# A hybrid recurrent layer on one core: the mixers' steps emitted by an estimated clock of each engine

## The chip, the core and the metric

The kernel runs on one core of a Trainium2 chip. The core has a matrix engine (TensorE, PE in the profile), a vector engine (VectorE, DVE), a scalar engine (ScalarE, ACT), a general engine (GpSimd, POOL) and SyncE (SP), whose queue issues most DMAs; each engine runs its own instructions in order and waits on the others through semaphores. The metric is the device time of one execution in microseconds.

## The reference

One layer on a prompt of 512 tokens and a sample of 64, model width 2048, all in float32. What is computed, cut to what matters:

```python
def gla_step(s, blk):                      # 4 heads, dk 128, dv 256
    q, k, v, g = blk
    big_g = jnp.cumsum(g, axis=2)
    ...
    attn = jnp.einsum('bhid,bhjd,bhijd->bhij', q, k, decay)
    o = (jnp.einsum('bhij,bhjv->bhiv', attn, v)
         + jnp.einsum('bhid,bhdv->bhiv', q * jnp.exp(big_g), s))
    ...
def gdn_step(s, blk):                      # 8 heads, dk = dv = 128
    q, k, v, g, beta = blk
    ...
    lower = jnp.where(strict, jnp.einsum('bhid,bhjd->bhij', kb, k) * decay, 0.0)
    sol = lax.linalg.triangular_solve(eye + lower, rhs, left_side=True, lower=True,
                                      unit_diagonal=True)
    u = sol[..., :dv] - jnp.einsum('bhik,bhkv->bhiv', sol[..., dv:], s)
    o = (jnp.einsum('bhid,bhdv->bhiv', q * jnp.exp(big_g)[..., None], s)
         + jnp.einsum('bhij,bhjv->bhiv', attn, u))
    ...
def trunk(x, c, states, params, block):
        mod = jax.nn.silu(c) @ w_ada[l] + b_ada[l]
        sh1, sc1, g1, sh2, sc2, g2 = jnp.split(mod[:, None, :], N_MOD, axis=-1)
        h = rmsnorm(x, norm1[l]) * (1 + sc1) + sh1
        mix, s_a, s_b, s_c = token_mixers(h, ...)   # h @ w_in, conv + silu on GDN's q/k/v,
                                                    # gla_step, gdn_step, norms, gates, @ w_out
        x = x + g1 * mix
        h = rmsnorm(x, norm2[l]) * (1 + sc2) + sh2
        f, s_f = conv_ffn(h, ...)                   # w_up, causal conv, silu * val, w_down
        x = x + g2 * f
```

## The kernel before

The stages follow each other on TensorE. The head (0 to 197 us) computes the first two modulation vectors, the norm and its transposes. Then come 50 tiles of the input projection, `gdn_heads` (31) and `gla_heads` (19); then the output projection, its second half of rows (k from 8) first; then the FFN and the last norm. Weights arrive in float32 (`raw`), ScalarE rounds them to `wh` and VectorE takes the rest as `wl` (L650 to L652); a product is three matmuls, high times high, low times high and high times low (L564, L566). Prompt and sample form 2 x 288 columns, so one *gemm step* is six matmuls of 128x288, and a tile has 16 steps.

After each gemm step `K.tick` runs, 928 times in all. A tick takes one step of the oldest job that has something to do, and steps of the modulation stream. A job is a generator: `gdn` for each delta-rule head (and one for the samples), `gla` for each gated head. It yields `WAIT` when it has nothing to issue. Before, it says how many ticks to wait by constants, such as these:

```python
REST_S, REST_L, REST_D, REST_X, REST_U, REST_T, REST_H, REST_N, REST_O, REST_G = 2, 3, 6, 4, 12, 2, 2, 4, 4, 4
LAG_CONV, LAG_COPY = 11, 5
ADA_AHEAD = 2
```

`gdn` transposes (L157), forms the strictly lower matrix (L227), and inverts it: `inverse16` writes it to DRAM (L372), reads the diagonal 16x16 blocks so that they lie on lanes (L378), eliminates them on POOL (a chain of 14 pairs), writes back (L389), reads (L393) and unpacks them on VectorE with a mask (L398). Two levels of matmuls (L249, then a mask product on VectorE, then L255 and an addition on VectorE), and for the heads a third (L263, L269), double the blocks; between two of them lies a *hop*, TensorE to VectorE and back, in which TensorE should have gemm steps to run. Norms add a constant on VectorE (L150) and raise to a power on POOL. `_Sooner` (L1710) gives the jobs' instructions a higher priority in the scheduler; `_InTurn` (L1725) keeps POOL's instructions in the order in which they were emitted. SP's queue holds weight loads (L650), modulation weight loads (L812), and the DRAM trips in the scheduler's order.

The modulation stream `ada_blocks` computes the four other modulation vectors on VectorE: 512 KB of `w_ada` (tile `aw`, L812), four multiply-adds on it (L848, L850), and after 8 loads a sum by TensorE (L822). It gets 0.72 of a step each tick, and its pauses use up steps too. `gdn_conv` (a convolution of four taps on VectorE, L990, and SiLU on ScalarE, L994) and `gla_gate` are called at once at the end of their projection tile, all their instructions together.

## Time and profile before

| | us |
|---|---|
| median of 3 runs (lowest, highest) | 2925.44 (2918.93, 2926.12) |
| the profiled execution | 2921.86 |
| its span, first to last instruction | 2920.1 |
| TensorE busy | 2823.8 (97%) |
| VectorE busy | 2051.2 (70%) |
| ScalarE busy | 1182.5 (40%) |
| GpSimd busy | 311.7 (11%) |

The granted clock of TensorE was 0.987 of full speed in the mean. All 128 loads of `aw`, 512 KB each, go through SP's queue. In the views `PE L255 <- POOL m L1725` reads: an instruction of line 255 on TensorE stood, and the last event before it started was POOL's on a tile named m, from line 1725. Buffers and names of one kind share a name (`m` is a pool of tiles of 128x512). A time in square brackets is the idle time of the engine before that instruction. `SPq` is SP's queue.

### The profile page before, as it was taken

Reading aid. Unit: us, or ns where it says so; the run is one execution under the profiler, and the core shown is the slowest. Engines: PE = TensorE matmul, PEld = TensorE weight load, DVE = VectorE, ACT = ScalarE, POOL = GpSimd, SP = SyncE. Lnnn points to the kernel's source line nnn. Section 1 sums busy time; section 2 is a strip of 40 time slices with the busy share of each in tenths; the row PEclk is TensorE's granted clock in tenths of the full one; section 3 lists DMA queues with packets and bytes.
Section 4 is the critical chain, followed back from the end, with each engine's and each line's share of the span. In section 5 each row is a group of like instructions: output and inputs, shape, how many; then the busy total and the mean of one; then the engine's idle time right before and its main releaser. Section 6 shows DMA issues by size and latency. Waiting matters only on the chain.

```text
span 2920.1 us, 52016 instructions
## 1 busy us (share of the span) xinstructions
PE 2823.8 (97%) x20964; PEld 2734.4 (94%) x20964; DVE 2051.2 (70%) x3299; ACT 1182.5 (40%) x2032; POOL 311.7 (11%) x513
## 2 busy tenths in 40 slices
PE   6999989999899999999999999999999999999998
PEld 3688889999899998999999999999999999999997
DVE  3368666777568787578888888888888855555555
ACT  4234534555454343255444444444444421222223
POOL 0005141222200000000111111111111100000000
PEclk8999999999999999999999999999999999999999
DMA  8865544555444548633333334333333553323221
GB/s 267 283 204 150 161 133 138 149 150 161 135 131 144 155 118 231 184 119 96 106 111 107 102 104 116 109 99 107 109 109 106 181 185 97 119 96 120 80 81 66
DMA packets 535444, 395.53 MB, mean 135 GB/s; under 512 B 59657, under 2 KB 465412, under 8 KB 535204
## 3 DMA queue, kind: packets, MB, share of 16 engines
q1 hardware_dynamic: 527860, 390.54, 44.7%
q8 instruction: 165, 2.70, 0.4%
q10 hardware_dynamic: 7344, 1.67, 0.3%
q14 instruction: 75, 0.61, 0.1%
HBM read 356.47 MB, written 35.67 MB: 134 GB/s over the span
## 4 chain that ended last, share of the span: by engine, by line
PE 80%; DVE 6%; POOL 4%; issue 4%; DMA 3%; ACT 2%; SPq 1%; ACTq 0%; POOLq 0%; DVEq 0%
PE g L564 26%; PE g L566 13%; PE bank L1388 11%; PE bank L1387 11%; PE bank L1389 11%; POOL m L1725 3%; DVE acc L850 1%; PE bank L724 1%; PE bank L157 1%; PE bank L441 1%; DVE wl L652 1%; DVE ca L990 1%; DVE m L1710 1%; ACT m L1710 1%; DMA d<-m 1%
## 5 line engine op out<-in xcount | busy, mean ns | idle before, releaser
L1388 PE MATMUL bank<-slot,wh 128*128 128x290 f32 x2464 | 737.3, 299 | 0.0
L1387 PE MATMUL bank<-slot,wh 128*128 128x290 f32 x2464 | 733.2, 298 | 0.0
L1389 PE MATMUL bank<-slot,wl 128*128 128x290 f32 x2464 | 728.2, 296 | 0.0
L564 PE MATMUL g<-slot,wh 128*128 128x288 f32 x3168 | 552.7, 295 | 0.2 <-DVE slot L1157 0.2
L564 PE MATMUL g<-hh,wh 128*128 128x288 f32 x2048 | 476.6, 313 | 1.0 <-ACT wh L651 1.0
L1389 PEld LDWEIGHTS bank<-slot,wl 128*128 128x128 f32 x2464 | 470.6, 191 | 0.0
L1388 PEld LDWEIGHTS bank<-slot,wh 128*128 128x128 f32 x2464 | 468.7, 190 | 0.1
L564 PEld LDWEIGHTS g<-slot,wh 128*128 128x128 f32 x3168 | 464.5, 188 | 0.7 <-DVE slot L1157 0.5
L1387 PEld LDWEIGHTS bank<-slot,wh 128*128 128x128 f32 x2464 | 463.6, 188 | 0.1
L651 ACT ACTIVATE wh<-raw 128x1024 fp32r<-128x1024 f32 x215 | 227.6, 1058 | 539.1 <-PE g L564 507.0
L564 PE MATMUL g<-hl,wh 128*128 128x288 f32 x2048 | 445.1, 298 | 0.0
L566 PE MATMUL g<-hh,wl 128*128 128x288 f32 x2048 | 443.7, 297 | 0.0
L1157 DVE SCALAR_TENSOR_TENSOR slot<-g,mod,slot 128x512 f32<-128x512 f32 (+1 forms) x448 | 201.6, 491 | 268.5 <-PE g L566 267.7
L564 PEld LDWEIGHTS g<-hh,wh 128*128 128x128 f32 x2048 | 328.4, 191 | 20.8 <-issue 16.3
L850 DVE SCALAR_TENSOR_TENSOR acc<-aw,ct,acc 128x512 f32<-128x512 f32 x480 | 337.7, 750 | 10.2 <-DMA aw<-in_w_ada_dram 10.2
L566 PE MATMUL g<-slot,wl 128*128 128x288 f32 x1584 | 342.6, 295 | 0.0
L566 PEld LDWEIGHTS g<-hh,wl 128*128 128x128 f32 x2048 | 331.6, 190 | 6.2 <-issue 6.2
L564 PEld LDWEIGHTS g<-hl,wh 128*128 128x128 f32 x2048 | 332.4, 190 | 3.6 <-issue 3.5
L652 DVE TENSOR_TENSOR wl<-raw,wh 128x1024 fp32r<-128x1024 f32 x215 | 262.6, 1222 | 64.6 <-ACT wh L651 64.0
L1334 ACT ACTIVATE wh<-raw 128x1024 fp32r<-128x1024 f32 x176 | 186.2, 1058 | 224.2 <-PE bank L1388 182.3
L566 PEld LDWEIGHTS g<-slot,wl 128*128 128x128 f32 x1584 | 256.1, 188 | 0.0
L1335 DVE TENSOR_TENSOR wl<-raw,wh 128x1024 fp32r<-128x1024 f32 x176 | 215.3, 1223 | 54.0 <-ACT wh L1334 54.0
(351 smaller groups left out, 3102.2 us busy)
## 6 DMA issues: line engine op xcount, KB each, us to landing
raw<-in_w_up_dram SPq DMA_DIRECT2D x176, 512.0 KB
aw<-in_w_ada_dram SPq DMA_DIRECT2D x128, 512.0 KB
raw<-in_w_in_dram SPq DMA_DIRECT2D x100, 512.0 KB
raw<-in_w_down_dram SPq DMA_DIRECT2D x88, 512.0 KB
hraw<-in_w_ada_dram SPq DMA_DIRECT2D x64, 512.0 KB
raw<-in_w_out_dram SPq DMA_DIRECT2D x32, 512.0 KB
slot<-actd SPq DMA_DIRECT2D x44, 288.0 KB
actd<-v SPq DMA_DIRECT2D x44, 256.0 KB
```

The source lines that it names most:

```text
L564: T.matmul(ps[:, h if bank is None else bank, :n], wh, x[:, h, :n], start=f, stop=False)
L566: T.matmul(ps[:, h if bank is None else bank, :n], wl, ah[:, h, :n], start=False, stop=stop)
L651: nc.scalar.activation(hi[:, :n_], raw[:, :n_], AF.Copy)
L652: nc.vector.tensor_tensor(lo[:, :n_], raw[:, :n_], hi[:, :n_].bitcast(F32), op=ALU.subtract)
L850: V.scalar_tensor_tensor(acc[s], w[:, k], col, acc[s], op0=ALU.mult, op1=ALU.add)
L1157: self.nc.vector.scalar_tensor_tensor(x1[:, :, z], ps[:, :, c], gain[:, q:q + 1], x1[:, :, z], op0=ALU.mult, op1=ALU.add)
L1334: self.nc.scalar.activation(hi, src, AF.Copy)
L1335: self.nc.vector.tensor_tensor(lo, src, hi.bitcast(F32), op=ALU.subtract)
L1387: T.matmul(ps, wh[:, j], hi, start=(c < 3 and j == 0), stop=False, skip_group_check=True)
L1388: T.matmul(ps, wh[:, j], lo, start=False, stop=False, skip_group_check=True)
L1389: T.matmul(ps, wl[:, j], hi, start=False, stop=(j == NPAIR - 1), skip_group_check=True)
L1725: r = f(*a, **kw)
```

## The change

Two constants for each engine (a fixed price and a price per element), 0.795 us for a gemm step and prices for a DMA make a planner's clock. `K.now` is TensorE's, `K.free` has the time at which each other engine should be through with what was emitted, and each job has a `chain`, the planned end of its last instruction. `until` yields `WAIT` until TensorE's clock has passed the chain, `hop` does so after a yield, `moved` puts a DMA's price on the chain, `wait_for` waits for a tile's planned time. All counts of ticks go. The four taps of `gdn_conv` and the parts of `gla_gate` become tasks that run over several ticks and call `done` with a planned time; the jobs wait for q and k by it. The modulation stream takes a step only while VectorE's planned backlog is below 1 us; credit of 0.72 a tick is kept, up to 200 steps, and waits use none. Its weights have two buffers in place of three, and the pool m 17 in place of 15. The GLA jobs and the samples start their steps once at most one GDN job is left. `_Sooner` and `_InTurn` stay.

```diff
-REST_S, REST_L, REST_D, REST_X, REST_U, REST_T, REST_H, REST_N, REST_O, REST_G = 2, 3, 6, 4, 12, 2, 2, 4, 4, 4
-REST_C = 11
-REST_V = 5
-LAG_CONV, LAG_COPY = 11, 5
-ADA_AHEAD = 2
+TICK_US, HOP_US, DMA_US, ISSUE_US = 0.795, 0.25, 2.6, 0.5
+ADA_BACKLOG, ADA_CREDIT = 1.0, 200.0
+OP_US = {"V": (0.12, 1 / 960.0), "A": (0.10, 1 / 960.0), "G": (0.30, 1 / 480.0)}
+ADA_AHEAD = 1
...
-        self.jv, self.ja = _Sooner(tc, tc.nc.vector), _Sooner(tc, tc.nc.scalar)
-        self.pool = _InTurn(tc, tc.nc.gpsimd)
+        self.now, self.chain, self.free = 0.0, None, dict.fromkeys(OP_US, 0.0)
+        self.jv, self.ja = _Timed(self, _Sooner(tc, tc.nc.vector), "V"), _Timed(self, _Sooner(tc, tc.nc.scalar), "A")
+        self.tv, self.ta = _Timed(self, tc.nc.vector, "V"), _Timed(self, tc.nc.scalar, "A")
+        self.jt = _TimedPE(self, tc.nc.tensor)
+        self.pool = _Timed(self, _InTurn(tc, tc.nc.gpsimd), "G")
...
+    def rsqrt_steps(self, out, src, n):
+        self.rsqrt(out, src, n)
+        yield from self.until()
...
-        yield from self.rest(REST_C)
+        yield from self.wait_for(x, "q")
+        yield from self.wait_for(x, "k")
...
-        self.rsqrt(rq, ss, 4)
+        yield from self.until()
+        yield from self.rsqrt_steps(rq, ss, 4)
         V.tensor_scalar_mul(rq, rq, float(P) ** -0.5)
-        yield from self.rest(REST_T)
+        self.chain = at
+        yield from self.hop()
...
-                yield from self.hop(0)
+                yield from self.hop()
...
+    def charge(self, key, n, extra=0.0):
+        base, per = OP_US[key]
+        start = max(self.free[key], self.now + HOP_US, self.chain or 0.0)
+        self.free[key] = end = start + base + per * n + extra
+        if self.chain is not None:
+            self.chain = end
+    def charge_pe(self, us):
+        self.now += us
+        if self.chain is not None:
+            self.chain = max(self.chain, self.now)
+    def wait_for(self, x, name):
+        while name not in x or self.now < x[name, "at"]:
             yield WAIT
-        V.tensor_tensor(kF, kF, x["gate"](), op=ALU.mult)
-        yield from self.rest(REST_O)
-        o_put(kF)
-    def ready(self, x, name):
-        return name in x and self.ticks >= x.get((name, "at"), 0)
-    def put_ready(self, x, name, get, lag):
-        x[name], x[name, "at"] = get, self.ticks + lag
+    def put_ready(self, x, name, get, at):
+        x[name], x[name, "at"] = get, at
...
-    def rest(self, n):
-        for _ in range(n):
+    def until(self):
+        while self.now < self.chain + HOP_US:
             yield WAIT
-    def hop(self, n=REST_H):
+    def hop(self):
         yield
-        yield from self.rest(n)
+        yield from self.until()
+    def moved(self, n=1):
+        self.chain = max(self.chain, self.now) + DMA_US + n * ISSUE_US
...
-        yield from self.rest(REST_S)
+        yield from self.until()
...
+        self.moved(4)
+        yield from self.until()
...
-        yield from self.rest(REST_X)
+        self.moved(2)
+        yield from self.until()
         t, u = self.m4(), self.m4()
         for w, x in enumerate((t, u)):
-            nc.vector.tensor_tensor(x.rearrange("p b (n j) -> p b n j", n=8), cm[:, w].unsqueeze(2).to_broadcast(sh),
+            self.tv.tensor_tensor(x.rearrange("p b (n j) -> p b n j", n=8), cm[:, w].unsqueeze(2).to_broadcast(sh),
                                     c["bd16"].rearrange("p (n j) -> p n j", n=8).unsqueeze(1).to_broadcast(sh), op=ALU.mult)
-        yield from self.rest(REST_U)
+        yield from self.hop()
...
+    def fewer(self, n):
+        while sum(j[0].__name__ == "gdn" for j in self.jobs) > n:
+            yield WAIT
+    def start(self, gen, at=0.0):
+        self.jobs.append([gen, max(at, self.now)])
+    def spawn(self, gen):
+        self.tasks.append([gen, self.now])
+        self.run_tasks(self.tasks[-1:])
+    def run_tasks(self, tasks):
+        for j in tasks:
+            self.chain = j[1]
+            done = next(j[0], self) is self
+            j[1], self.chain = self.chain, None
+            if done:
+                self.tasks.remove(j)
     def tick(self):
-        self.ticks += 1
+        self.now += TICK_US
         self.run_due()
+        self.run_tasks(list(self.tasks))
         self.at_job += JOB_RATE
         while self.at_job >= 1:
             self.at_job -= 1
             self.job_step()
-        self.at_ada += ADA_RATE
-        while self.at_ada >= 1:
+        self.at_ada = min(self.at_ada + ADA_RATE, ADA_CREDIT)
+        while self.at_ada >= 1 and self.free["V"] - self.now < ADA_BACKLOG:
+            r = next(self.ada, self)
+            if r is self or r is WAIT:
+                break
             self.at_ada -= 1
-            next(self.ada, None)
     def job_step(self):
-        for g in list(self.jobs):
-            r = next(g, self)
+        for j in list(self.jobs):
+            self.chain = j[1]
+            r = next(j[0], self)
+            j[1], self.chain = self.chain, None
             if r is self:
-                self.jobs.remove(g)
+                self.jobs.remove(j)
             if r is not WAIT:
                 return
...
-        V = self.nc.vector
+        V = self.tv
         todo = [(blk, k0) for blk in blocks for k0 in range(0, KD, 2)]
         got = []
         for n, (blk, k0) in enumerate(todo):
             while len(got) < min(len(todo), n + 1 + ADA_AHEAD):
                 got.append(self.ada_load(*todo[len(got)], lambda: self.ap.tile([P, 1024], F32, tag="aw", bufs=1 + ADA_AHEAD, name=self.name("aw"))))
                 if n == 0:
-                    yield
+                    yield WAIT
...
-                yield from self.rest(4)
+                yield from self.pause(self.free["V"] + HOP_US)
...
-    def gdn_conv(self, ps, t, dst, name, h):
-        nc = self.nc
-        V, A = nc.vector, nc.scalar
+    def gdn_conv(self, ps, t, dst, name, h, done):
...
+        end = self.chain
         V.tensor_copy(self.cs[:, :, :, t], cb[:, 512:646].rearrange("p (s c) -> p s c", s=2)[:, :, 0:3])
+        self.chain = end
+        yield from self.until()
         A.activation(dst, acc[:, 0:512], AF.Silu)
+        end = self.chain
         self.put_s(name, h, lambda s: A.activation(s, acc[:, 515:579], AF.Silu))
+        done(end + HOP_US)
...
+            self.spawn(self.gdn_conv(ps, 8 * n + h, t, "qkv"[n], h, lambda at: self.put_ready(x, "qkv"[n], lambda: b4(t), at)))
...
+        self.free["A"] += 2.6
+        self.chain += 2.6
+        yield from self.until()
...
+            self.spawn(self.gla_gate(h, g.rearrange("p b t -> p (b t)"), gated))
+            self.start(self.gla(4, *qk, g, x, None, o["p_gla"][0, 0, h], lambda f, t, h=h: self.put_o(2 * h + f, t)))
...
+class _Timed:
+    def __init__(self, k, engine, key):
+        self.k, self.engine, self.key = k, engine, key
+    def __getattr__(self, name):
+        f = getattr(self.engine, name)
+        def g(*a, **kw):
+            out = kw["out"] if "out" in kw else a[0]
+            self.k.charge(self.key, _size(out), 0.2 if "accum_out" in kw else 0.0)
+            return f(*a, **kw)
+        return g
...
+    def matmul(self, out, *a, **kw):
+        self.k.charge_pe(0.22 * max(1.0, _size(out) / P))
+        return self.engine.matmul(out, *a, **kw)
...
-    BUFS = {"m": 15, "qkv": 8, "gt": 3}
+    BUFS = {"m": 17, "qkv": 8, "gt": 3}
```

Instruction counts are the same on PE, VectorE, POOL and for the DMAs; ScalarE loads its table 46 times where it did 48 times. Three places show how the order moves.

TensorE, the first head's inverse: `bank<-m` is a matmul of a level, `g<-hh,wh` and the like are gemm steps (three rows a step). Before:

```order
L249 MATMUL bank_381_2740<-m_375_2635,m_317_2176 128x64 x4
L564 MATMUL g_385_2754<-hh_85_550,wh_387_2756 128x288 x2
L564 MATMUL g_385_2754<-hl_86_551,wh_387_2756 128x288 x2
L566 MATMUL g_385_2754<-hh_85_550,wl_388_2757 128x288 x2
L564 MATMUL g_385_2754<-hh_89_562,wh_387_2756 128x288 x2
L564 MATMUL g_385_2754<-hl_90_563,wh_387_2756 128x288 x2
L566 MATMUL g_385_2754<-hh_89_562,wl_388_2757 128x288 x2
L564 MATMUL g_385_2754<-hh_94_581,wh_387_2756 128x288 x2
L564 MATMUL g_385_2754<-hl_95_582,wh_387_2756 128x288 x2
L566 MATMUL g_385_2754<-hh_94_581,wl_388_2757 128x288 x2
L255 MATMUL bank_389_2785<-m_307_2091,m_374_2634 128x64 x4
```

After (L633 and L635 are the gemm's lines, L1850 the heads' matmuls):

```order
L1850 MATMUL bank_398_2896<-m_390_2854,m_336_2375 128x64 x4
L633 MATMUL g_394_2865<-hh_138_865,wh_396_2867 128x288 x2
L633 MATMUL g_394_2865<-hl_139_866,wh_396_2867 128x288 x2
L635 MATMUL g_394_2865<-hh_138_865,wl_397_2868 128x288 x2
L633 MATMUL g_394_2865<-hh_142_877,wh_396_2867 128x288 x2
L633 MATMUL g_394_2865<-hl_143_878,wh_396_2867 128x288 x2
L635 MATMUL g_394_2865<-hh_142_877,wl_397_2868 128x288 x2
L1850 MATMUL bank_400_2924<-m_306_2071,m_389_2853 128x64 x4
```

Between the first matmul of the level and the one that needs VectorE's product stand two gemm steps where three stood.

POOL, the elimination of the third head (tile `m_403_2947` before, `m_393_2863` after); `s8...mhalf` is the power function of an older head's norm. Before:

```order
L1725 TENSOR_TENSOR m_403_2947<-m_403_2947 32x13x2 x2
L1725 TENSOR_TENSOR m_403_2947<-m_403_2947 32x12x3 x2
L1725 TENSOR_TENSOR m_403_2947<-m_403_2947 32x11x4 x2
L1725 TENSOR_TENSOR s8_552_3904<-s8_552_3904,mhalf_98 128x4
L1725 TENSOR_TENSOR m_403_2947<-m_403_2947 32x10x5 x2
L1725 TENSOR_TENSOR m_403_2947<-m_403_2947 32x9x6 x2
L1725 TENSOR_TENSOR m_403_2947<-m_403_2947 32x8x7 x2
```

After:

```order
L1864 TENSOR_TENSOR m_393_2863<-m_393_2863 32x11x4 x2
L1864 TENSOR_TENSOR m_393_2863<-m_393_2863 32x10x5 x2
L1864 TENSOR_TENSOR m_393_2863<-m_393_2863 32x9x6 x2
L1864 AFFINE_SELECT m_571_4059<-m_571_4059 128x512
L1864 AFFINE_SELECT m_570_4058<-m_570_4058 128x512
L1864 TENSOR_TENSOR m_393_2863<-m_393_2863 32x8x7 x2
L1864 TENSOR_TENSOR s8_566_4036<-s8_566_4036,mhalf_98 128x4
L1864 TENSOR_TENSOR m_393_2863<-m_393_2863 32x7x8 x2
L1864 TENSOR_TENSOR m_393_2863<-m_393_2863 32x6x9 x2
L1864 TENSOR_TENSOR m_393_2863<-m_393_2863 32x5x10 x2
```

The power function still stands inside the chain, some pairs later, and two mask fills of the next head stand there too; each is emitted when its input should be ready by plan.

SP's queue around the write-back of the same head (`d1<-m`), with weight loads (`raw`), modulation weight loads (`aw`) and the reads of the blocks (`cm`). Before:

```order
L320 DMA out_3_dram<-st_547_3883 128x128
L812 DMA aw_565_4044<-in_w_ada_dram 128x2x512
L389 DMA d1_491_3504<-m_403_2947 32x2x256
L812 DMA aw_570_4096<-in_w_ada_dram 128x2x512
L999 DMA od9_72<-qkv_336_2349 256x1x256
L393 DMA cm_569_4086<-d1_491_3504 128x4x16 x2
```

After:

```order
L881 DMA aw_576_4098<-in_w_ada_dram 128x2x512
L324 DMA out_3_dram<-st_561_4006 128x128
L881 DMA aw_577_4138<-in_w_ada_dram 128x2x512
L719 DMA raw_626_4533<-in_w_in_dram 128x8x128
L422 DMA d1_528_3809<-m_393_2863 32x2x256
L881 DMA aw_588_4281<-in_w_ada_dram 128x2x512
L427 DMA cm_599_4350<-d1_528_3809 128x4x16 x2
```

Ahead of the write-back a projection load has come in between it and the modulation load; between the write-back and the reads one modulation load stands in both, and the store of a finished head (`od`) no longer does.

206 lines of the change are left out of this document (127 added, 79 removed).

## The prediction

> **What bounds the kernel.** I read the stages first, then what TensorE waits for, then the queues behind the longest waits. Busy time by stretch (start:end, length, then each engine's busy time with its instruction count, granted clock, DMA share, GB/s):
>
> ```profile
> 197.00:814.00 617.00, 578.15 (x4413) 562.84 (x4412) 435.94 (x805) 305.99 (x763) 175.85 (x314) 0.97 0.52 149
> 814.00:1098.00 284.00, 281.90 (x2100) 267.59 (x2100) 223.17 (x450) 126.62 (x245) 12.90 (x20) 1.00 0.48 139
> 1098.00:1330.00 232.00, 227.98 (x1690) 220.18 (x1689) 158.50 (x265) 95.86 (x174) 6.73 (x24) 1.00 0.58 169
> ```
>
> TensorE bounds all three. It is idle for 617 - 578.15 = 38.9 us while the GDN heads run (197 to 814), 2.1 us in the GLA heads and 4.0 us in the first part of the output projection, 45.0 us together. The change touches no stage behind them. What TensorE waited for in the first (us in all, times, longest):
>
> ```profile
> PE bank L255 <- POOL m L1725: 14.0, 2, 7.8
> PE bank L157 <- DVE m L1710: 7.3, 3, 6.4
> PE bank L157 <- ACT qkv L994: 5.1, 2, 2.6
> PE bank L249 <- DVE m L398: 4.8, 2, 4.6
> PE bank L157 <- ACT qkv L1131: 3.3, 1, 3.3
> PE bank L255 <- DVE m L1710: 1.9, 3, 1.0
> PE bank L269 <- DVE m L1710: 1.5, 1, 1.5
> ```
>
> Hops of the inverse (L249, L255, L269, and L157 on m) are 14.0 + 7.3 + 4.8 + 1.9 + 1.5 = 29.5 us; tiles written by ScalarE are 5.1 + 3.3 = 8.4; about 1 us is in smaller rows.
>
> A second loss follows the long gaps: TensorE runs at half clock for a while. These are the first and fourth of six such stretches, and the sum over the six:
>
> ```profile
> 276.40:280.10 3.70, 3.66 (x16) 3.69 (x17) 3.70 (x6) 0.00 (x0) 3.30 (x6) 0.50 0.51 150
> ...
> 614.60:618.00 3.40, 3.40 (x16) 3.38 (x17) 0.00 (x0) 3.37 (x10) 1.23 (x2) 0.50 0.60 218
> ...
> sum 27.00, PE 25.14 PEld 24.73 DVE 21.02 ACT 4.88 POOL 7.82; mean PE 4.19 PEld 4.12 DVE 3.50 ACT 0.81 POOL 1.30
> ```
>
> 25.14 us of work at half speed is 12.6 us lost. All that the change can win is 45.0 + 12.6 = 57.6 us.
>
> **Where the gaps come from.** The first, at 276 us, on VectorE and TensorE:
>
> ```profile
> 271.24 4.72 DVE L850 SCALAR_TENSOR_TENSOR acc<-aw,ct,acc 128x512 f32<-128x512 f32 x7
> 275.88 0.42 DVE L1710 TENSOR_TENSOR m<-bank,consts 128x256 f32<-128x256 f32 x1
> ...
> 276.44 1.94 PE L255 MATMUL bank<-m,m 128*128 128x64 f32 x8 [6.10 <-POOL m L1725]
> ```
>
> The view names POOL, but the tile that arrived last is VectorE's mask product at 275.88, queued behind seven modulation steps. The second, at 297 us, is VectorE standing 8.8 us for the diagonal blocks that come back through DRAM:
>
> ```profile
> 296.40 0.69 DVE L398 TENSOR_TENSOR m<-cm,consts 128x512 f32<-128x512 f32 x1 [8.83 <-DMA cm<-d]
> 297.01 0.41 DVE L1710 TENSOR_TENSOR m<-m,bank 128x256 f32<-128x256 f32 x1
> ...
> 297.48 1.11 PE L157 MATMUL bank<-consts,m 128*128 128x128 f32 x4 [6.37 <-DVE m L1710]
> ```
>
> The third, at 423 us, starts on POOL 40 us earlier (POOL, SP's queue, VectorE, TensorE):
>
> ```profile
> 382.86 1.18 POOL L1725 TENSOR_TENSOR s<-s,mhalf 128x4 f32<-128x4 f32 x1 [23.82 <-DVE s L150]
> 384.02 14.70 POOL L1725 TENSOR_TENSOR m<-m 32x50 f32<-32x50 f32 x20
> ...
> 384.52 0.37 SPq L812 DMA_DIRECT2D aw<-in_w_ada_dram  x1
> 399.42 0.33 SPq L389 DMA_DIRECT2D d<-m  x1
> 399.80 1.09 SPq L812 DMA_DIRECT2D aw<-in_w_ada_dram  x1
> 401.62 1.28 SPq L393 DMA_DIRECT2D cm<-d  x2
> ...
> 404.54 2.08 DVE L850 SCALAR_TENSOR_TENSOR acc<-aw,ct,acc 128x512 f32<-128x512 f32 x3 [5.89 <-DMA aw<-in_w_ada_dram]
> 406.54 1.29 DVE L398 TENSOR_TENSOR m<-cm,consts 128x512 f32<-128x512 f32 x2
> ...
> 423.07 1.94 PE L255 MATMUL bank<-m,m 128*128 128x64 f32 x8 [7.85 <-POOL m L1725]
> ```
>
> An older head's power function was queued inside the next head's elimination chain, 23.8 us before its input existed. The chain stood, the write-back (L389) stood on it, and the weight loads (L812) queued behind the write-back came late; VectorE stood 5.9 us and caught up just ahead of a hop. Over the run these two waits sum to (SP's queue, then POOL):
>
> ```profile
> SPq L389 <- POOL m L1725: 86.5, 9, 15.8
> POOL s L1725 <- DVE s L150: 484.2, 17, 85.1
> ```
>
> **The change, part by part.** No engine gets work or loses any but two ACT table loads, so the price is all in waits. The busy rows that give the prices: first the modulation step over the whole span, then the groups of 197 to 1098 us, the last a table load on ScalarE:
>
> ```profile
> L850 DVE SCALAR_TENSOR_TENSOR acc<-aw,ct,acc 128x512 f32<-128x512 f32 x480 | 337.7, 750 | 10.2 <-DMA aw<-in_w_ada_dram 10.2
> ...
> L850 DVE SCALAR_TENSOR_TENSOR acc<-aw,ct,acc 128x512 f32<-128x512 f32 x420 | 296.6, 751 | 8.0 <-DMA aw<-in_w_ada_dram 8.0
> L652 DVE TENSOR_TENSOR wl<-raw,wh 128x1024 fp32r<-128x1024 f32 x97 | 119.0, 1227 | 50.5 <-ACT wh L651 50.2 <-DMA qkv<-early_aq 0.3
> L990 DVE SCALAR_TENSOR_TENSOR ca<-conv_in,cols,ca 128x579 f32<-128x579 f32 x72 | 58.9, 818 | 2.4 <-ACT ca L988 1.9
> L398 DVE TENSOR_TENSOR m<-cm,consts 128x512 f32<-128x512 f32 x18 | 12.1, 686 | 31.8 <-DMA cm<-d 31.8
> L1710 DVE TENSOR_TENSOR m<-bank,consts 128x256 f32<-128x256 f32 (+1 forms) x23 | 10.7, 467 | 13.2 <-PE bank L249 13.0 <-PE bank L417 0.2
> ...
> L994 ACT ACT_TABLE_LOAD x11 | 14.1, 1283 | 0.2
> ```
>
> *Hops, 29.5 us before.* A modulation step is now emitted only while VectorE's planned backlog is under 1 us, so seven in a row ahead of a hop (gap one) should not recur. But a hop gets about two gemm steps of TensorE work as cover where it had three. A step is six matmuls at a pitch of 0.133 us, 0.8 us, so 1.6 in place of 2.4 (the first pairs of two steps that follow each other after the first hop, 0.79 us apart):
>
> ```profile
> 268.58 0.43 PE L564 MATMUL g<-hh,wh 128*128 128x288 f32 x2
> ...
> 269.37 0.43 PE L564 MATMUL g<-hh,wh 128*128 128x288 f32 x2
> ```
>
> A hop with one modulation step and one weight split still ahead takes 0.47 + 0.75 + 1.23 = 2.45 us and leaves 0.85 open; with only one of them it is covered. There are 52 hops (8 heads and the samples with two levels of two, and a last level of two in the heads), so 0 to 52 * 0.85 = 44 us. L850 and L652 fill 416 of 901 us, 46%; both ahead, 0.46 squared or 21%: 11 hops, 10 us (an estimate that treats the two as independent).
>
> *Blocks through DRAM (L398), inside the 29.5.* VectorE no longer unpacks by a count of ticks but after a planned landing. Planned from the write-back: 2.6 + 0.5, then 2.6 + 1.0, 6.7 us; the row shows 399.42 to 406.54, 7.1. The elimination before it is planned at one pair of instructions each tick (14 pairs, 11 us); at 14.70 / 20 = 0.735 us each, 28 take 20.6. So the plan can still be early, by 0 to 10 us a head, and SP's queue, which keeps its order, then stands on the write-back with the block loads and at least one weight load behind it. Of the 31.8 us that VectorE stood here I leave half, 16, and of that a quarter on TensorE, 4 us (bounds 0 and 6.4 + 4.6 = 11, the two longest gaps after L398). The power functions now wait for their squares by plan; gap three goes, except for what the late chain leaves.
>
> *Convolutions as tasks, 8.4 us before.* The transposes of v wait for a planned end, which leaves out the SiLU's table load: three late tiles of 1.28 us, 4 us (bounds 0 and 8.4).
>
> *Two weight buffers in place of three.* The load of the next half megabyte starts when VectorE frees the buffer, one step group (four L850, 3.0 us) ahead of its use, against two. In the rows above a load issued at 399.80 was used at 404.54, 4.7 us. Each load could leave 1.7 us, but VectorE has heads' work between: from 0 to 120 loads (480 steps, four a load) * 1.7 = 204 us of its own idle time, which lies beside TensorE unless a hop stands behind it. I take the nearest row, the 8.0 us of L850 in this stretch, as 10 of idle, of which 3 reach TensorE.
>
> *Tails.* In TensorE's order the last modulation sum comes after 828 of 928 gemm steps where it came after 910, the last GLA head some 30 steps later than before, still 87 steps ahead of the half projection that needs it. The FFN is untouched. I leave 2.1 + 4.0 and the 1 us of small rows: 7 us.
>
> *Clock.* Six half-clock stretches become two of 3.4 us, 3.4 us lost (0 to 12.6). This row, a gap of 2.63 us, stands right before the stretch at 614.60 above:
>
> ```profile
> 614.54 1.10 PE L157 MATMUL bank<-consts,qkv 128*128 128x128 f32 x4 [2.63 <-ACT qkv L994]
> ```
>
> The Trainium skill, "TensorE: Matmul & The Clock Gate" (Part 1, what's actually happening), says that the clock halves after at least one idle window of about 3.4 us. By it gaps under 3.4 us would cost no clock, this term would be 0 and the sum 3 us lower. The trace disagrees, since 2.63 us sufficed, and the sum goes by the trace.
>
> *Sum.* Left: 10 + 4 + 4 + 3 + 7 + 3.4 = 31.4; gained 57.6 - 31.4 = 26.2 us. The profiled execution took 2921.86 us (span 2920.1), 3.6 under the median of 2925.44. So 2895.7 for such an execution, 2899 against the median. The range of this case is 2872 to 2917: with only the tails' 7 left it would be 2875, and the lowest run before lies some us under its median; above, the next case begins.
>
> **Rivals.** *The waits only move* (0.18). Twice the hops overrun (20 us), L398 keeps its 11, the convolutions their 8.4, the weight buffers cost 8 and the clock 8: left 62 with the tails, 5 us slower (2930), and with any of them smaller somewhat faster: 2917 to 2934. The change would then not do what it says: its plan moves the steps, but not to where their inputs are ready. For it: the cover of a hop is shorter by a third. Against: 814 to 1098 has VectorE 79% busy and TensorE idle for only 2.1 us.
>
> *VectorE becomes the bound: slower* (0.20). The plan prices an instruction on VectorE at 0.12 us + elements / 960: L850 0.653 against 0.751, L990 0.723 against 0.818, L652 1.187 against 1.227. Over 480, 72 and 97 that is 47 + 7 + 4 = 58 us which the planner believes free. If it fills VectorE by its own clock, the backlog it thinks is under 1 us grows, TensorE waits the 58, with 10 for the weight buffers and 12.6 of half clock: 81 in place of 57.6, some 23 us slower, 2948. It decides once VectorE's true load passes about 95%. Against: its load in the two head stages is 659 of 901 us; with the 60 steps (480 - 420, 45 us) that move in from the projection 704 of some 875, 80%.
>
> **How the numbers follow.** Forecast 0.62, moved waits 0.18, VectorE-bound 0.20. I call under 0.3% (8.8 us) no change: faster is below 2916.7, slower above 2934.2. The three cases fall on the three sides: 0.62, 0.18, 0.20. The range reaches from 2872 to 2936, through the moved waits and to the edge of the slower case.
>
> **What the profile after would show.** Right: TensorE idle in the GDN stage about 20 us in place of 38.9; no run of seven L850 instructions before a mask product; POOL's wait for the norm's input far below 484 us; one or two half-clock stretches. Wrong: VectorE over 90% busy in that stage, waits of L850 for its weights above 20 us, or TensorE's waits on m above 25 us.

## The result: no change

The changed kernel takes 2924.93 us (median of 12 runs, 2922.49 to 2927.05), the kernel before, run beside it, 2924.34 us. The ratio is 1.0006, with a 95% interval of 0.9998 to 1.0013: nothing gained and nothing lost, where a gain of 26 us was forecast. The profiled execution has a span of 2923.0 us against 2920.1.

**The profile after.** Busy time by stretch, as for the kernel before:

```profile
197.00:814.00 617.00, 575.29 (x4379) 560.16 (x4378) 462.90 (x845) 300.71 (x746) 164.06 (x283) 0.96 0.53 154
814.00:1098.00 284.00, 280.67 (x2122) 269.69 (x2120) 230.09 (x457) 124.89 (x253) 24.73 (x55) 1.00 0.52 152
1098.00:1330.00 232.00, 228.43 (x1662) 220.74 (x1663) 122.59 (x207) 95.46 (x174) 5.52 (x17) 0.99 0.48 138
```

TensorE is idle for 41.7 us in the GDN stage where it was for 38.9, and VectorE is busy for 462.9 us there where it was for 435.9. Seven stretches at half clock hold 39.16 us of TensorE work where six held 25.14:

```profile
286.30:300.00 13.70, 8.73 (x39) 8.40 (x38) 11.26 (x18) 8.04 (x15) 11.40 (x23) 0.50 0.54 155
...
1102.10:1108.90 6.80, 6.53 (x27) 6.18 (x28) 5.49 (x8) 1.14 (x3) 0.00 (x0) 0.50 1.14 315
sum 57.90, PE 39.16 PEld 38.47 DVE 44.72 ACT 15.04 POOL 12.84; mean PE 5.59 PEld 5.50 DVE 6.39 ACT 2.15 POOL 1.83
```

The long waits of before are gone, and others stand in their place. What TensorE waits for from 197 to 1340 us, then what VectorE, SP's queue and POOL wait for up to 1100 us:

```profile
PE bank L1850 <- DVE st L1810: 15.3, 5, 7.5
PE bank L1850 <- DVE m L1810: 12.8, 4, 6.2
PE bank L1850 <- DVE sq L1810: 10.5, 3, 8.1
PE g L633 <- ACT wh L1834: 3.7, 1, 3.7
```

```profile
DVE acc L1834 <- DMA aw<-in_w_ada_dram: 39.8, 18, 7.9
```

```profile
SPq L422 <- POOL m L1864: 91.6, 9, 13.8
```

```profile
POOL s L1864 <- DVE s L1834: 256.6, 15, 39.1
```

VectorE no longer stands on the blocks that come back through DRAM (31.8 us before, no such row now), and POOL's wait for the older head's norm fell from 484 to 257 us. But VectorE stands 39.8 us on its modulation weights (10.2 before), and the waits on `st` and `sq`, tiles of the heads' state loop, are all but new (0.5 us before). SP's wait on POOL is much as it was (86.5 us before).

**One of the new gaps.** SP's queue, POOL, VectorE and TensorE before 451 us:

```profile
431.67 0.37 SPq L719 DMA_DIRECT2D raw<-in_w_in_dram  x1
442.42 0.33 SPq L422 DMA_DIRECT2D d<-m  x1
442.84 0.38 SPq L881 DMA_DIRECT2D aw<-in_w_ada_dram  x1
```

```profile
423.40 16.06 POOL L1864 TENSOR_TENSOR m<-m 32x14 f32<-32x14 f32 x24
439.42 1.22 POOL L1864 TENSOR_SCALAR_AFFINE_SELECT m<-m 128x512 f32<-128x512 f32 x2
440.62 1.10 POOL L1864 TENSOR_TENSOR m<-m 32x26 f32<-32x26 f32 x4
```

```profile
437.62 1.40 DVE L1834 SCALAR_TENSOR_TENSOR acc<-aw,ct,acc 128x512 f32<-128x512 f32 x2
446.94 2.74 DVE L1834 SCALAR_TENSOR_TENSOR acc<-aw,ct,acc 128x512 f32<-128x512 f32 x4 [7.92 <-DMA aw<-in_w_ada_dram]
449.60 1.22 DVE L1834 TENSOR_TENSOR wl<-raw,wh 128x1024 fp32r<-128x1024 f32 x1
450.74 0.28 DVE L1810 COPY st<-bank 128x128 f32<-128x128 f32 x1
```

```profile
451.07 0.79 PE L1850 MATMUL bank<-st,qkv 128*128 128x128 f32 x2 [7.48 <-DVE st L1810]
```

POOL's elimination takes 19 us. SP's queue reaches the write-back (L422) at 432 us and stands there for 10 us. A modulation load stands behind it. VectorE, in order, uses up the weights it has, stands 7.9 us, and behind the modulation steps stands the copy of a head's state on which TensorE waits. The gaps at 607 and 692 us (6.0 and 8.1 us) have the same build, each just behind an L422 that SP issued late (at 599.49 and 684.31 us):

```profile
605.53 0.75 DVE L1834 SCALAR_TENSOR_TENSOR acc<-aw,ct,acc 128x512 f32<-128x512 f32 x1 [7.41 <-DMA aw<-in_w_ada_dram]
606.59 0.79 PE L1850 MATMUL bank<-st,qkv 128*128 128x128 f32 x2 [6.00 <-DVE st L1810]
...
690.43 1.41 DVE L1834 SCALAR_TENSOR_TENSOR acc<-aw,ct,acc 128x512 f32<-128x512 f32 x2 [7.49 <-DMA aw<-in_w_ada_dram]
692.16 0.80 PE L1850 MATMUL bank<-sq,m 128*128 128x128 f32 x2 [8.05 <-DVE sq L1810]
```

The three gaps are 21.5 us together. The half-clock stretches behind them hold 5.8 + 3.9 + 3.7 us of TensorE work and so cost 6.7 us more: 28 us, about as much as the gain that was forecast. The gap at 566 us (6.2 us) is another thing: VectorE paused only 0.9 us in the 6 us before it, and was running modulation steps ahead of the hop.

### The profile page after: what moved, and what is told of

Read it like the earlier page. It is cut to its first block, busy times and chain, and to the rows that moved or that the text cites. A ratio compares the mean times of both kernels' runs of the same rounds, so it can differ in the third digit from the quotient of the medians.

```text
span 2923.0 us, 51988 instructions
## 1 busy us (share of the span) xinstructions
PE 2823.2 (97%) x20964; PEld 2738.8 (94%) x20964; DVE 2053.8 (70%) x3299; ACT 1178.5 (40%) x2030; POOL 312.4 (11%) x513
## 4 chain that ended last, share of the span: by engine, by line
PE 75%; POOL 3%; DVE 3%; DMA 2%; issue 2%; ACT 1%; SPq 0%; ACTq 0%; POOLq 0%; DVEq 0%
PE g L633 24%; PE g L635 12%; PE bank L1487 11%; PE bank L1486 11%; PE bank L1488 11%; PE bank L1850 3%; POOL m L1864 3%; DVE acc L1834 1%; DMA aw<-in_w_ada_dram 1%; PE bank L1846 1%; DVE wl L1834 0%; PE bank L1696 0%; DMA raw<-in_w_down_dram 0%; DVE m L1810 0%; DVE ca L1834 0%
## 5 line engine op out<-in xcount | busy, mean ns | idle before, releaser
L633 PE MATMUL g<-slot,wh 128*128 128x288 f32 x3168 | 552.7, 295 | 0.2 <-DVE slot L1834 0.2
L633 PE MATMUL g<-hh,wh 128*128 128x288 f32 x2048 | 476.1, 313 | 3.7 <-ACT wh L1834 3.7
L633 PEld LDWEIGHTS g<-slot,wh 128*128 128x128 f32 x3168 | 464.5, 188 | 0.7 <-DVE slot L1834 0.5
L635 PE MATMUL g<-hh,wl 128*128 128x288 f32 x2048 | 446.5, 299 | 0.0
L633 PE MATMUL g<-hl,wh 128*128 128x288 f32 x2048 | 446.1, 299 | 0.0
L1834 ACT ACTIVATE wh<-raw 128x1024 fp32r<-128x1024 f32 x215 | 227.1, 1056 | 538.0 <-PE g L633 530.8
L1834 DVE SCALAR_TENSOR_TENSOR slot<-g,mod,slot 128x512 f32<-128x512 f32 (+1 forms) x448 | 201.6, 491 | 305.4 <-PE g L635 304.6
L1834 DVE SCALAR_TENSOR_TENSOR acc<-aw,ct,acc 128x512 f32<-128x512 f32 x480 | 343.0, 751 | 40.1 <-DMA aw<-in_w_ada_dram 39.8
L633 PEld LDWEIGHTS g<-hh,wh 128*128 128x128 f32 x2048 | 328.7, 192 | 23.0 <-issue 16.3
L635 PE MATMUL g<-slot,wl 128*128 128x288 f32 x1584 | 342.6, 295 | 0.0
L635 PEld LDWEIGHTS g<-hh,wl 128*128 128x128 f32 x2048 | 334.2, 191 | 6.2 <-issue 5.9
L633 PEld LDWEIGHTS g<-hl,wh 128*128 128x128 f32 x2048 | 334.3, 191 | 3.4 <-issue 3.4
L1834 DVE TENSOR_TENSOR wl<-raw,wh 128x1024 fp32r<-128x1024 f32 x215 | 262.9, 1223 | 22.5 <-ACT wh L1834 22.1
L635 PEld LDWEIGHTS g<-slot,wl 128*128 128x128 f32 x1584 | 256.1, 188 | 0.0
```

The lines of the kernel that those rows point to most:

```text
L633: T.matmul(ps[:, h if bank is None else bank, :n], wh, x[:, h, :n], start=f, stop=False)
L635: T.matmul(ps[:, h if bank is None else bank, :n], wl, ah[:, h, :n], start=False, stop=stop)
L1834: return f(*a, **kw)
```

## The experiments

Two theories stood against the plain one that waits only move. **A**: late modulation weights, from SP's wait on POOL and two buffers. **C**: too low a price on VectorE, so that modulation steps are let in where there is no time. **B** is the rival of the prediction: a gap that goes comes back at another step.

The first table gives the times. The second, worked out from the traces, compares a kernel with the kernel before where TensorE has done the same work (each matmul counted with the usual pitch of its kind): the columns are times of the kernel before, the entries how much later (or, negative, earlier) the other has got so far, in us. The profiled execution of the kernel before took 3.6 us less than the median of its first three runs, so the entries are some us in its favour. They are rough. e5, e13 and e16 issue the same instructions up to 850 us, and their entries at 524 us still differ by 5.7 us, so that much lies between two executions; and another price for the small matmuls moves single entries, those at 740 and 861 us most, by up to 5 us. The expectations on record count by gemm steps, by which leads look larger (21 us in one case), since some of the heads' matmuls were still to come at that step.

| label | median us | ratio to before (95%) | VectorE's wait on aw |
|---|---|---|---|
| changed kernel | 2924.93 | 1.0006 (0.9998 to 1.0013) | 39.8 |
| e4_before_two | 2940.36 | 1.0053 (1.0038 to 1.0068) | 41.1 |
| e1_three_buffers | 2939.15 | 1.0048 (1.0031 to 1.0065) | 13.2 |
| e8_three_buffers_b | 2936.89 | 1.0038 (1.0023 to 1.0052) | 12.2 |
| e11_three_buffers_c | 2923.43 | 0.9995 (0.9984 to 1.0005) | 9.6 |
| e2_pool_queue | 2954.77 | 1.0102 (1.0087 to 1.0117) | 9.1 |
| e3_both | 2968.01 | 1.0145 (1.0130 to 1.0160) | none |
| e7_late_writeback | 2924.70 | 1.0005 (0.9995 to 1.0015) | 53.5 |
| e5_vector_price | 2939.66 | 1.0056 (1.0038 to 1.0074) | 31.3 |
| e6_no_catch_up | 2964.79 | 1.0138 (1.0113 to 1.0162) | 52.7 |
| e9_price_870 | 2941.64 | 1.0054 (1.0037 to 1.0072) | 64.7 |
| e10_price_870_late | 2942.17 | 1.0053 (1.0036 to 1.0070) | 59.0 |
| e12_buffers_and_price | 2953.89 | 1.0094 (1.0073 to 1.0116) | 13.3 |
| e13_price_820_late | 2920.80 | 0.9989 (0.9979 to 0.9999) | 26.3 |
| e14_price_820_buffers | 2926.91 | 1.0003 (0.9993 to 1.0012) | 9.2 |
| e15_price_820_later | 2926.30 | 1.0002 (0.9993 to 1.0011) | 23.5 |
| e16_price_820_earlier | 2914.04 | 0.9960 (0.9946 to 0.9974) | 25.8 |
| e17_price_820_600 | 2917.44 | 0.9972 (0.9961 to 0.9983) | 30.5 |

| at | 524 | 635 | 740 | 861 | 964 | 1067 | 1173 | 1274 |
|---|---|---|---|---|---|---|---|---|
| changed kernel | -5.7 | 4.9 | 13.9 | 5.2 | 4.1 | 2.9 | 6.1 | 5.7 |
| e4_before_two | 13.5 | 13.8 | 15.5 | 16.9 | 18.5 | 20.3 | 20.3 | 21.1 |
| e11_three_buffers_c | -8.3 | -4.0 | 6.9 | 0.5 | 3.9 | 2.7 | 6.0 | 5.5 |
| e5_vector_price | -6.7 | -6.2 | -1.0 | -16.2 | -9.3 | -10.5 | -14.7 | 18.8 |
| e6_no_catch_up | 2.2 | 10.7 | 22.9 | 7.2 | 7.4 | 9.7 | 7.6 | 46.0 |
| e9_price_870 | 2.7 | 8.4 | 32.2 | 15.6 | 22.3 | 28.5 | 23.8 | 23.7 |
| e12_buffers_and_price | -10.1 | -8.6 | -2.0 | 7.6 | 27.1 | 35.1 | 41.7 | 41.1 |
| e13_price_820_late | -6.9 | -6.4 | -1.7 | -17.4 | -9.0 | -9.9 | -13.1 | -1.3 |
| e14_price_820_buffers | -12.8 | -11.5 | -10.3 | -14.4 | 0.1 | -1.0 | -3.8 | 8.0 |
| e16_price_820_earlier | -1.2 | -0.4 | 4.4 | -11.3 | -1.8 | -3.4 | -2.0 | -2.0 |

The changed kernel is ahead at first, loses 20 us between 524 and 740 in the three gaps at 566, 607 and 692 us, and gets 9 back where the kernel before has its own late gaps (763 to 798 us).

### Two buffers in the kernel before

```diff
-ADA_AHEAD = 2
+ADA_AHEAD = 1
```

> The kernel before with two weight buffers in place of three and nothing else. Theory A: the loads behind SP's wait on POOL (86.5 us) come too late here too, VectorE's waits on aw rise from 10 to about 40 us, some 20 us of them reach TensorE: about 2945 us. Rival B: VectorE's waits for weights lie beside TensorE, 2925 us within 9.

One third of the weight buffers less costs the kernel before 14.6 us (2940.36 against 2925.77 beside it). Its own trace shows why, in VectorE's waits:

```profile
DVE acc L850 <- DMA aw<-in_w_ada_dram: 41.1, 23, 10.7
```

This bears out one half of A: the change gives up the third buffer for two more tiles of the pool m, and giving it up, done alone to the kernel before, has this price (A had about 20 us). Whether the changed kernel would be as much faster with its third buffer back is what the next runs ask.

### Three buffers in the changed kernel

The third buffer needs 4 KB a partition, and room came from other pools, by three ways.

```diff
-ADA_AHEAD = 1
+ADA_AHEAD = 2
...
-    BUFS = {"m": 17, "qkv": 8, "gt": 3}
+    BUFS = {"m": 17, "qkv": 8, "gt": 2}
```

All three have the edit above; besides, e1 cuts the sample state tiles `s0` from 4 to 2; e8 cuts `s0`, `sq` and `ts` from 4 to 3 each; e11 cuts the GLA state tiles `sl` and the 1 KB tiles `qc` from 3 to 2 each.

> The changed kernel with three weight buffers for the modulation stream again (room for it comes from two gate tiles in place of three and two sample state tiles in place of four). Theory A: in the changed kernel SP's queue stands on the write-back of the elimination, the modulation loads behind it come late, and with two buffers VectorE stands on them (39.8 us, 18 times), with a head's step behind; three of TensorE's gaps (7.5, 6.0 and 8.1 us) are this, and with the half-clock stretches behind them (5.8 + 3.9 + 3.7 us of work at half speed, 6.7 us lost) they cost 28 us. By it VectorE's waits on aw fall to about 10 us, those three gaps go, and the time is about 2897 us. Rival B: VectorE is too full for the shorter hops and a gap that goes comes back at the next step; the time stays within 9 us of 2925.

> Three weight buffers in the changed kernel again, with the room from elsewhere, because two tiles for the sample states cost TensorE 6.4 us of waits and half-clock stretches behind them in the samples' steps: two gate tiles in place of three, three state tiles in place of four, three small tiles in place of four. Without the samples' waits Rival B expects 2925 us within 9 (the gaps come back elsewhere, as they did with the other three buffers); Theory A, 2900 us.

> The changed kernel with three weight buffers, the room from tiles that the samples' GDN steps do not use (two gate tiles in place of three, two GLA state tiles in place of three, two of the 1 KB tiles in place of three). With the two other ways of making room TensorE had done 51 and 89 matmuls more by 814 us (7 and 12 us of work) and lost it in the samples' steps. Theory A: that gain is kept, about 2913 us. Rival B: within 9 us of 2925, with gaps at other steps.

VectorE's wait on weights fell to 9.6 to 13.2 us in all three, as A said, but the time did not fall. e1 and e8 lie above the ranges of both theories: the smaller pools put new waits into the samples' steps (2.41 us on a state load and 2.94 us on `ts` in e1, with a half-clock stretch of 13.7 us). In e11, without most of these, the kernel is 9 us ahead of the changed kernel at 635 us and level with it from 964 us on. Its larger gaps:

```profile
450.27 0.80 PE L1850 MATMUL bank<-sq,m 128*128 128x128 f32 x2 [6.67 <-DVE sq L1810]
...
709.07 1.94 PE L1850 MATMUL bank<-m,m 128*128 128x64 f32 x8 [4.17 <-DVE m L1810]
...
846.92 1.08 PE L1850 MATMUL bank<-qc,m 128*128 128x64 f32 x8 [3.06 <-DVE m L1810]
```

The first is the gap at 451 us of the changed kernel, and it is a late weight still: SP stood 14 us on POOL there, and three buffers did not last that long.

```profile
444.12 0.33 SPq L422 DMA_DIRECT2D d<-m  x1
...
448.54 1.42 DVE L1834 SCALAR_TENSOR_TENSOR acc<-aw,ct,acc 128x512 f32<-128x512 f32 x2 [6.17 <-DMA aw<-in_w_ada_dram]
```

The gap at 607 us shrank to 2.0 us and the one at 692 us went, with its wait for weights. In their place came one of 2.9 us at 690 us, on a modulation sum's copy, and the two others shown: the one at 709 us has no counterpart in the changed kernel, and the nearest to the one at 847 us is of 1.1 us there. So a third buffer takes away most of the late weights and, in the end, no time. e11 came out in B's range; whether the smaller pools have a part in the new gaps was not separated.

### POOL's own queue

```diff
-        nc.sync.dma_start(d1.rearrange("w q f -> q w f"), lane)
+        G.engine.dma_start(d1.rearrange("w q f -> q w f"), lane)
...
-            nc.sync.dma_start(cm[:, w], d1[w].rearrange("(b n) (i j) -> (n i) b j", b=4, i=16))
+            for h in range(0, 4, 2):
+                G.engine.dma_start(cm[:, w, h:h + 2], d1[w, 8 * h:8 * h + 16].rearrange("(b n) (i j) -> (n i) b j", b=2, i=16))
```

This is e2; e3 has the edits of e1 besides.

> The changed kernel (two weight buffers), with the write-back of the elimination and the reads of the blocks issued from POOL's own queue in place of SP's (the reads as four DMAs in place of two). Theory A: SP no longer stands on POOL (91.6 us before), the modulation loads are issued when their buffer is free, VectorE's waits on aw fall from 39.8 to about 10 us and the three gaps go: about 2897 us. Rival B: within 9 us of 2925. If the second buffer alone is the cause, whatever SP does, the waits on aw stay above 30 us here and go only with three buffers.

> Both edits together. Theory A: the two take away the same wait from two sides, so little is left for the second: 2890 to 2897 us. Rival B: within 9 us of 2925.

SP stopped waiting on POOL, and the weights came (9.1 us, then none). Yet both kernels are slower, outside the ranges of A and of B: the trip itself became longer. POOL's queue in e2, the first head:

```profile
277.64 0.75 POOL L1865 DMA_DIRECT2D d<-m  x1 [0.32 <-POOL m L1865]
280.44 0.73 POOL L1865 DMA_DIRECT2D cm<-d  x1 [2.05 <-DMA d<-m]
284.04 0.73 POOL L1865 DMA_DIRECT2D cm<-d  x1 [2.87 <-issue]
...
288.77 0.73 POOL L1865 DMA_DIRECT2D cm<-d  x1 [1.66 <-issue]
```

From the first of the four reads to the last it takes 8 us, where SP issued its two in 0.92 us (at 444 us in the changed kernel), and VectorE, whose plan had 6.7 us for the whole trip, stands on the blocks again:

```profile
DVE m L1835 <- DMA cm<-d: 50.6, 13, 5.3
```

As a test of A this is spoiled by its own cost; it only shows that SP's wait can be exchanged for a dearer one.

### A later write-back

```diff
         G.tensor_copy(xt, xx.rearrange("p i j -> p j i"))
+        self.chain += 8.0
```

> The changed kernel with 8 us added to the planned end of each elimination on POOL, which takes 17 to 19 us where the plan has 11. Theory A: the write-back is issued when POOL is through, so SP's wait on POOL falls from 91.6 to under 30 us, VectorE's waits on aw from 39.8 to under 15, and the three gaps go: about 2900 us. Theory C: the queues ahead of the hops stay, 2918. Rival B: within 9 us of 2925; the heads also end 8 us later each, which costs nothing while the projection needs them later still.

SP's wait on POOL did not fall (109.8 us), VectorE's waits on aw rose, the time is the same. The eight microseconds did not bring SP to the write-back any later: in the mean of the nine, SP was through with the DMA before it 5.7 us after POOL had begun the elimination, where that was 11.3 us in the changed kernel. So the run is no test of A. Why SP's order came out like this was not followed further.

### VectorE's price, and the pace

```diff
-OP_US = {"V": (0.12, 1 / 960.0), "A": (0.10, 1 / 960.0), "G": (0.30, 1 / 480.0)}
+OP_US = {"V": (0.12, 1 / 820.0), "A": (0.10, 1 / 960.0), "G": (0.30, 1 / 480.0)}
```

is e5; e6 instead sets `ADA_CREDIT` from 200.0 to 2.0.

> The changed kernel with VectorE priced as measured: 0.12 us + elements / 820 in place of / 960, so a modulation step is 0.744 (measured 0.751) in place of 0.653. Theory C: the plan thinks VectorE free when it is not, lets modulation steps in, and nine or so of them stand ahead of a hop; with the right price the queues ahead of the hops (gaps of 5.0 and 6.2 us) go and with them a part of the others: about 2908 us. Theory A (late weight loads behind SP's wait on POOL) expects no more than 5 us from it, since the waits on aw stay. Rival B (a gap that goes comes back at another step): within 9 us of 2925.

> The changed kernel with a credit for modulation steps of at most 2 in place of 200, so that the stream never runs faster than 0.72 of a step each tick to make up for a pause. Theory C: VectorE is less full in the stretches with much of the heads' work, fewer steps stand ahead of a hop: about 2908 us, with the stream ending later. Theory A: the loads are asked for less fast, so the waits on aw fall from 39.8 to about 25 us and the time to about 2915. Rival B: within 9 us of 2925.

e5 ends later than the kernel before, but at 1173 us it is 14.7 us ahead of it. The modulation steps of the GDN stage, in the changed kernel and in e5:

```profile
L1834 DVE SCALAR_TENSOR_TENSOR acc<-aw,ct,acc 128x512 f32<-128x512 f32 x333 | 238.9, 754 | 37.7 <-DMA aw<-in_w_ada_dram 37.4
```

```profile
L1834 DVE SCALAR_TENSOR_TENSOR acc<-aw,ct,acc 128x512 f32<-128x512 f32 x279 | 198.9, 747 | 19.7 <-DMA aw<-in_w_ada_dram 19.5
```

The changed kernel runs 333 of them there, e5 279 and the kernel before 300. What C said would go went only in part: its gap of 5.0 us at 294 us is one of 3.4 us in e5, and that of 6.2 us at 566 us is still 5.8 us, with five modulation steps in a row ahead of the hop. What went are the three gaps of A; one of 6.0 us came at 315 us, behind a wait of 7.3 us for weights. TensorE's waits in e5 up to 1200 us:

```profile
PE bank L1850 <- DVE m L1810: 23.8, 8, 6.0
PE bank L1850 <- POOL m L1864: 8.2, 2, 4.8
...
PE bank L1850 <- DVE sq L1810: 0.7, 1, 0.7
```

The waits on `st` and `sq`, 25.8 us in the changed kernel, are 0.7 us, and those on m have doubled, from 16.0 to 32.0 us. Yet e5 has two buffers too, and SP stands as long on POOL (89.3 us, up to 13.7 us at a time). So with the same stands and the same two buffers late weights cost one gap here and three there; where a stand falls against the stream would explain it, which was not tested. Fewer steps alone are not the reason: e6 runs only 258 there, and has gaps of 12.4 and 11.2 us behind waits for aw of 12.5 and 10.4 us. Why e5's order avoids most of the late weights is open.

The end is the other side. Of all steps on aw, 50 in e5 run after 1173 us, 17 in the kernel before and none in the changed one. They stand at the end of the projection's first part, where nothing covers them:

```profile
1229.59 1.64 PE L897 MATMUL bank<-acc,consts 128*32 128x256 f32 x8 [17.88 <-DVE acc L1834]
...
1242.74 1.33 PE L633 MATMUL g<-slot,wh 128*128 128x288 f32 x4 [10.34 <-ACT wh L1834]
```

It lost 33 us there. e6 ends the same way (24.2 and 9.3 us of waits), without the lead. So the price matters, though not by the way that C named, and the stream's end has a cost that the change did not have to pay.

e9 has `/ 870.0` in the first of these edits; e10 also allows a backlog of 3 us once no `gdn` job is left; e12 is e10 with the three buffers of e11.

> The changed kernel with VectorE priced at 0.12 us + elements / 870: a modulation step 0.709 us, between the changed kernel's 0.653 and the measured 0.751. At / 820 TensorE had done 137 matmuls more by 814 us (18 us of work), and lost it all at the end of the projection's first part, where the last modulation steps, not fitted in earlier, kept it waiting 17.9 + 10.3 us with a long half-clock stretch behind them. With this price the whole stream fits in before that place. Theory C (too low a price lets too many modulation steps in ahead of the hops): no such tail, and 9 to 18 us gained before 814 us: about 2910 us. Rival B (a gap that goes comes back at another step, since VectorE has the same work to do in less time): within 9 us of 2925.

> The same price, and a backlog of up to 3 us in place of 1 once no job of a GDN head is left, so that the stream ends earlier. Theory C: as with the price alone, 2910 us, with the tail safer. Rival B: within 9 us of 2925; the steps now stand ahead of the GLA jobs' steps instead.

> Three weight buffers, with the same room, the price of / 870 and the backlog of 3 us once no GDN job is left. If late weights and too many modulation steps are two causes that add up, about 2900 us. If they are the same lost time, 2910. Rival B: within 9 us of 2925.

These three lie above the ranges of all theories. In e9 no gap stands at the end of the projection's first part any more, and the kernel is 15 us slower than the kernel before, not 15 faster: VectorE waits longer for its weights (64.7 and 59.0 us on aw in e9 and e10), and in e9 TensorE has gaps of 9.6 and 12.0 us behind single waits of 9.3 and 12.9 us. The price does not act in proportion: with 960, 870 and 820 the entries at 1173 us are 6.1, 23.8 and -14.7. With three buffers besides (e12) the weights come, the kernel is 9 us ahead at 635, and loses all of that and more from 740 on, most of it in the GLA stage, where a modulation sum, a sample tile and a projection tile's copy now hold TensorE for 7.2, 4.6 and 4.4 us. That loss has several parts, the room taken from other tiles among them, which were not separated.

### The price, and all steps fitted in

```diff
-        while self.at_ada >= 1 and self.free["V"] - self.now < ADA_BACKLOG:
+        while self.at_ada >= 1 and self.free["V"] - self.now < (ADA_BACKLOG if self.now < 620 else 3.0):
```

with `/ 820.0` is e16; e13 has 650 and 2.0, e15 700 and 3.0, e17 600 and 2.0; e14 is e13 with the three buffers of e11.

> VectorE at its measured price (/ 820), as in the run that was 16 us ahead of the kernel before when 996 gemm steps were done, and 18 us behind 100 steps later, since 28 modulation steps were left over. Here the allowed backlog of VectorE is 2 us in place of 1 once the plan's clock is past 650 us, where the GLA heads are nearly through, and all steps fit in before the end. Theory C (the changed kernel's price lets VectorE fill beyond what it can do): the lead is kept, 2905 to 2912 us. Rival B (what is taken from one place is lost at another): the denser stream costs the lead again, 2917 to 2934.

> The same with three weight buffers, the room as in the third of the runs with them. If the late weights are a cause of their own beside the price: some 8 us below the run before, 2897 to 2905. If not: the same as that run, or, by Rival B, 2917 to 2934.

> The first of these with the backlog of 3 us from 700 us of the plan's clock on. Theory C: like the first, 2905 to 2912 us, if the steps that are left for the end are few enough for the gaps of the projection's first part. Rival B: 2917 to 2934.

> VectorE at its measured price, backlog 3 us from 620 us of the plan's clock on, so that the modulation stream ends at 933 us of the plan where it ended at 948 in the run with 650. That run was 21 us ahead of the kernel before at 896 gemm steps and lost all but 2 of it by 1096, most of it at one wait of 8.7 us and the half-clock stretch behind it where the stream's last sum held up the second half of the projection. If that tail is where the gain goes, this kernel keeps 8 to 15 us: 2910 to 2917 us. If the denser stream costs as much ahead of it, 2921 to 2927.

> The same with a backlog of 2 us from 600 us of the plan's clock on; the stream ends at 938 us of the plan. If the tail is where the gain goes, between the other two: 2912 to 2919 us. If not, 2921 to 2927.

e13, e14 and e15 came out in the range of rival B and not of C. e13 carries a lead of 13 us to 1173 us and drops most of it by 1274 us, at one wait for the output projection's weights. They stand in SP's queue behind loads for which buffers come free only after the stream's last sum (1212 us):

```profile
1222.79 1.33 PE L633 MATMUL g<-slot,wh 128*128 128x288 f32 x4 [8.68 <-ACT wh L1834]
```

Ending the stream some 15 us of plan earlier removes that wait (nothing is lost between 1173 and 1274), and e16 takes 2914.04 us, 0.4% under the kernel before and 11 us under the changed kernel; e17, in between by plan, is in between by time. Both came out as written; e16 is the best of four settings of these two numbers. Part of what the end cost is now paid in the GLA stage: e16's lead falls there from 11 us to 2. By its profiled execution, 5 us under that of before, it gains less than by the medians, 12 us; the medians decide. e16's busy time shows the first stage better than before (28.9 us idle against 38.9), the second worse (9.8 against 2.1) and the third almost without idle time (0.5 against 4.0):

```profile
197.00:814.00 617.00, 588.12 (x4515) 575.30 (x4514) 432.46 (x804) 305.56 (x766) 146.33 (x294) 0.97 0.51 144
814.00:1098.00 284.00, 274.23 (x2023) 262.38 (x2022) 226.63 (x437) 124.41 (x236) 20.93 (x45) 0.98 0.55 158
1098.00:1330.00 232.00, 231.51 (x1717) 222.70 (x1716) 168.66 (x293) 97.54 (x185) 7.37 (x20) 1.00 0.57 164
```

A third buffer on top (e14) helps as far as 740 us (9 us ahead of e13) and costs as much by 964.

## Why the prediction was wrong

The sum forecast 31.4 us of loss left of 57.6. TensorE's idle time in the three stages and its half-clock loss come to 41.7 + 3.3 + 3.6 + 39.16 / 2 = 68 us. (The profiled spans differ by 2.9 us and not by 68 - 57.6 = 10.6, so this count is good to some 8 us.) By terms:

| term | forecast, us | in the trace after, us |
|---|---|---|
| hops | 10 | 17.1 |
| blocks through DRAM (L398) | 4 | 3.2 |
| convolutions | 4 | 1.4 |
| two weight buffers | 3 | 21.5 |
| tails and small rows | 7 | 5.4 |
| clock | 3.4 | 19.6 |

- *Two weight buffers, 3 us.* This is the step that failed. It took 10 us of idle time on VectorE from the row before, "of which 3 reach TensorE"; the trace after has 39.8 us on VectorE and, in three of TensorE's four largest gaps, 21.5 us on TensorE. The prediction had the pieces (a load issued behind the write-back, used 4.7 us later, against a lead of 3.0 us), but took the lateness as 1.7 us a load, when the loads that matter wait for SP to get past the write-back, up to 13.8 us at a time. The sign of being wrong that it named, waits of the modulation steps for their weights above 20 us, came. It also held that idle VectorE time lies beside TensorE "unless a hop stands behind it"; at 451, 607 and 692 us a head's state step stood behind it. Done alone to the kernel before, two buffers cost 14.6 us. In the changed kernel no run isolates the term: the third buffer took away three quarters of VectorE's waits and no time (e11), and with another price, and two buffers still, the three gaps went and another came (e5).
- *Clock, 3.4 us.* 39.16 / 2 = 19.6 us, with seven half-clock stretches where two were forecast. 6.7 us of it stand behind the three gaps above, so it follows in part from the same step.
- *Hops, 10 us.* TensorE's waits on m, `st` and `sq` are 12.8 + 3.2 + 15.3 + 10.5 = 41.8 us. Half of it is the late weights (21.5), 3.2 the unpacked blocks, and of the 17.1 left 11.2 are the gaps of 5.0 and 6.2 us behind VectorE's queue. Seven modulation steps in a row did not recur, but ahead of the gap of 5.0 us VectorE still ran seven between 285.9 and 293.0 us, with a split, two copies and a wait for weights of 1.0 us among them. What the shorter cover of two gemm steps costs by itself was not tested.
- *The rival "the waits only move"* (0.18) had the time, 2917 to 2934, but not by its sum: it had 11 for L398, 8.4 for the convolutions, and 8 each for the weight buffers and the clock. That the total fits is luck; its idea, that a gap that goes comes back at another step, fits e11, and e5, where the waits on m doubled.
- *The rival "VectorE becomes the bound".* VectorE was not the bound of the stage (462.9 of 617 us, 75%), so the price did not cost 58 us. Its premise, that the planner believes VectorE freer than it is, did show: in the GDN stage the plan ran 33 modulation steps more than before, 25 us of them, where heads compete for the engine.
- *Blocks through DRAM, 4 us.* VectorE no longer waits for the blocks, as forecast; TensorE waits 3.2 us for the unpacked tile (`m` of L1834). *Convolutions, 4 us*: 1.4 us is left, and that is a wait for a copied projection tile, as 3.3 of the 8.4 us before were (L1131).
- *The write-back.* "SP's queue, which keeps its order, then stands on the write-back" held (91.6 us), and the lateness of POOL, 19 us for a plan of 11, was seen, but its price was put on L398 alone and not on the weight loads.
- *Tails.* The stream ended early and cost nothing, as said. e5, e6 and e13, which run fewer steps in the GDN stage, paid at the end for what was left over.

## What to carry to other kernels

A queue that keeps its order passes a wait on. Here the loads behind the write-back came as late as POOL was, and a plan that priced the write-back's own reader alone missed that. How many buffers bridge such a stand has to be read against the longest stand and not the mean load: three did not bridge one of 14 us, and how much two cost changed with the order. A background stream that fills "free" time should be tried at its measured price, and its end looked after as well; the best kernel here (e16, 0.4% under the kernel before) has both. But the effect is not smooth: a price half way was worse than the wrong one. Read the progress of the bound engine step by step, not the end time alone, since a lead of 13 to 15 us was twice lost in one place; and compare two executions of the same instructions first, which here differ by 6 us.
